# Values of two head groups in the second layer: computed in the order of positions, then reordered through memory

## The chip, the cores and the metric

One core of one Trainium2 chip runs the whole kernel. The metric is the device time of one execution in microseconds (us), of which the median of several runs is taken. TensorE (PE in the rows) does the matmuls, and each has a weight load ahead of it (PEld) that puts the 128x128 stationary operand into the array. VectorE is DVE, ScalarE is ACT, GpSimd is POOL, and SP is the queue from which this kernel issues all its transfers (DMA).

## The reference, cut to what matters

Four layers on 1024 positions of width 1024: gated linear attention, dilated sliding-window attention, differential attention and latent attention. The change is in the second. There the keys and values of three groups of heads come from the layer's input `x`, and each group attends on an interleaved subsequence of the positions:

```python
SWA_GROUPS = ((128, 1), (512, 4), (2048, 16))   # window, dilation
...
kv = x @ w_kv
k, v = jnp.split(kv, [SWA_KV_HALF], axis=-1)
...
def to_strided(t):        # t = i*d + r: subsequence r holds every d-th position
    ...
    t = t.reshape(bsz, n_sub, dilation, t.shape[2], e).transpose(0, 2, 1, 3, 4)
    return t.reshape(bsz, dilation, nb, blk, t.shape[3], e)
...
o = jnp.einsum('brngpqk,brnkge->brnqgpe', p, vcat) / ...
```

So group 0 wants the values of its 128-position blocks in plain order, group 1 those of every 4th position, and group 2 those of every 16th (the kernel takes every 8th, and masks half of them).

## The kernel before

Activations are held transposed: `xh` and `xl` are the two halves (high and low part) of the layer's input, 128 rows of the width on the partitions and the 1024 positions along the free dimension, for 8 slices `kt` of the width. A product in full precision is three matmuls, in `mm3` (lines 165 to 167): high by high, high by low, low by high.

The values are made by `u_v`: a block of 128 positions is the **stationary** operand (128x128, loaded into the array by PEld), and the weights `wvhi`, `wvlo` of the group (256 columns, two heads) are the moving one. A block takes 8 slices x 3 = 24 matmuls, and its result, 128 positions x 256, goes from PSUM (tile `mm`, two buffers) into `Vt[g][:, st, :]` by VectorE or ScalarE (line 953). For groups 1 and 2 `vsel` picks the block's 128 positions out of `x` with a step of 4 or 8 floats, so the stationary operand is read from SBUF with that step.

TensorE's order is the order in which the program is written (`manual_schedule`). It comes from `Fill`, a list of units that are cut into pieces and given out against a budget of time: three gate units, group 0's first four blocks and half of group 1's blocks run beside the tail of the boundary before (`before.tail`, a layer norm that writes the second 512 positions of `xh` and `xl`). Then come group 0's blocks 4 to 7, `ada[0]`, group 1's other four, `ada[1]`, group 2's first four, `ada[2]`, group 2's last four, `ada[3]`. An `ada` unit loads 2048 KB (`xa`, two buffers, line 554), weights it on VectorE into `xb` in eight steps (lines 563 and 565), sums it by two matmuls (line 571) and takes the result out on VectorE (lines 574 to 577).

The order on the other engines is set by a scheduler at build time. Every transfer stands in SP's queue, and one that waits there holds up all behind it. When the pool of the value stage (`swv`) is closed, the tables `C` and `Sn` (lines 975 and 976) of the rotation are loaded, and beside them a chain of small jobs starts: `xb<-in_lam` (617), `xb<-in_positions` (639), the tables of the third layer on VectorE (lines 642 to 658), and eight means of output weights (`wo`, lines 595 to 603, loaded, centred and stored one after the other in one buffer). The units of keys and queries then run; their results are rotated by VectorE from PSUM (line 899: `t<-mm,C`, which frees the PSUM buffer).

## Time and profile before

| | |
|---|---|
| median of 3 runs | 2852.13 us (2846.84 to 2853.86) |
| profiled execution | 2852.29 us, of which the span from the first to the last instruction is 2850.5 us |
| busy share of the span | PE 95%, PEld 80%, DVE 66%, ACT 47%, POOL 11% |
| mean granted TensorE clock | 0.983 of full speed |
| transfers | 270.51 MB, mean 95 GB/s |
| single steps on VectorE in the value stage | line 563 0.49 us, line 565 0.75, line 574 0.69, line 576 0.69, a block's copy out of PSUM (line 953) 0.42, a low part of weights (line 150, 128x512) 0.69 |

Busy shares are means over four layers with different limits. A row of the timeline gives the start in us from the span's start, the duration, the engine, the line of the source, the operation and the tiles (out<-in), and in brackets how long the engine stood idle before it and what ended that. Matmuls are pipelined, so the duration of one is longer than the distance to the next; the distance is what counts.

### The profile page before, as it was taken

To read this page: it belongs to the slowest core of one execution; us is meant where nothing else is said; L and a number is where in the kernel's file an instruction comes from. 1 tells how busy PE (TensorE), PEld (TensorE's weight loads), DVE (VectorE), ACT (ScalarE), POOL (GpSimd) and SP (SyncE) were. 2 spreads that over 40 slices of the span, in tenths; PEclk is the share of its full clock that TensorE was granted. 3 is DMA by queue.
4 is the path that set the end of the run, shared out by engine and by line. 5 is a ranking of instruction groups with operands and counts; after the bars stand their busy time and mean duration, and the time that the engine had idled before them with its cause. 6 is when DMAs were issued, how large, how long until landed. Compare 5 with 4: busy or idle time off the path is not lost.

```text
span 2850.5 us, 39300 instructions
## 1 busy us (share of the span) xinstructions
PE 2719.8 (95%) x14788; PEld 2287.2 (80%) x14788; DVE 1892.6 (66%) x3486; ACT 1347.4 (47%) x2498; POOL 314.5 (11%) x224
## 2 busy tenths in 40 slices
PE   8999999999999999989899999998899999999998
PEld 6889887898778878867787787876678778888888
DVE  5766647546666666666676688887676527776784
ACT  4443345404444434445714666665546514554563
POOL 0000000000000000000005566665100000000000
PEclk9999999999999999999999999999899999999999
DMA  5311146513211111145453333342185121110143
GB/s 178 115 41 45 45 150 203 187 71 137 87 49 42 49 53 45 45 156 169 162 207 106 53 59 61 69 65 50 44 299 181 48 93 32 29 29 29 39 168 108
DMA packets 161575, 270.51 MB, mean 95 GB/s; under 512 B 32773, under 2 KB 79141, under 8 KB 159849
## 3 DMA queue, kind: packets, MB, share of 16 engines
q1 hardware_dynamic: 161384, 268.00, 30.6%
q8 instruction: 116, 1.90, 0.3%
q14 instruction: 75, 0.61, 0.1%
HBM read 193.38 MB, written 64.07 MB: 90 GB/s over the span
## 4 chain that ended last, share of the span: by engine, by line
PE 63%; DVE 15%; DMA 8%; ACT 7%; issue 4%; SPq 2%; POOL 1%; ACTq 0%; DVEq 0%; POOLq 0%
PE mm L166 14%; PE mm L165 14%; PE mm L167 14%; PE pt L1226 3%; PE sc L1643 2%; PE sc L1406 2%; PE sc L1035 2%; DVE den L1410 1%; PE lv L477 1%; DMA zt<-zt 1%; PE pt L1139 1%; PE sc L166 1%; ACT whi L192 1%; PE sc L165 1%; PE sc L167 1%
## 5 line engine op out<-in xcount | busy, mean ns | idle before, releaser
L165 PE MATMUL mm<-xh,whi 128*128 128x512 f32 x1472 | 621.7, 422 | 12.7 <-ACT xh L763 4.3
L167 PE MATMUL mm<-xh,wlo 128*128 128x512 f32 x1472 | 582.3, 396 | 2.8 <-POOL wlo L150 1.8
L166 PE MATMUL mm<-xl,whi 128*128 128x512 f32 x1472 | 582.9, 396 | 1.7 <-DVE xl L150 1.7
L165 PEld LDWEIGHTS mm<-xh,whi 128*128 128x128 f32 x1472 | 281.9, 192 | 71.5 <-ACT xh L763 7.0
L167 PEld LDWEIGHTS mm<-xh,wlo 128*128 128x128 f32 x1472 | 280.3, 190 | 65.4 <-POOL wlo L150 2.2
L166 PEld LDWEIGHTS mm<-xl,whi 128*128 128x128 f32 x1472 | 281.5, 191 | 53.7 <-DVE xl L150 4.0
L150 POOL TENSOR_TENSOR wlo<-wraw,whi 128x1024 fp32r<-128x1024 f32 x29 | 70.4, 2427 | 1407.5 <-ACT whi L192 1406.8
L165 PE MATMUL mm<-wvhi,xh 128*128 128x256 f32 x704 | 220.2, 313 | 3.6 <-DVE V L953 3.0
L167 PE MATMUL mm<-wvhi,xl 128*128 128x256 f32 x704 | 215.0, 305 | 0.1
L166 PE MATMUL mm<-wvlo,xh 128*128 128x256 f32 x704 | 214.9, 305 | 0.0
L192 ACT CAST whi<-wraw 128x1024 fp32r<-128x1024 f32 (+2 forms) x141 | 135.9, 964 | 131.4 <-PE mm L166 124.8
L1412 ACT ACTIVATE P<-sc,den 128x1024 f32<-128x1024 f32 x128 | 142.8, 1116 | 105.5 <-DVE den L1410 105.5
L165 PEld LDWEIGHTS mm<-wvhi,xh 128*128 128x128 f32 x704 | 153.6, 218 | 8.4 <-DVE V L953 3.2
L166 PEld LDWEIGHTS mm<-wvlo,xh 128*128 128x128 f32 x704 | 153.8, 219 | 0.9 <-issue 0.7
L1410 DVE TENSOR_REDUCE den<-sc 128x1 f32<-128x1024 f32 x128 | 153.6, 1212 | 1.4 <-PE sc L1406 1.4
L167 PEld LDWEIGHTS mm<-wvhi,xl 128*128 128x128 f32 x704 | 153.6, 218 | 0.5 <-DVE xl L150 0.5
L150 DVE TENSOR_TENSOR wlo<-wraw,whi 128x1024 fp32r<-128x1024 f32 (+2 forms) x113 | 123.5, 1093 | 43.0 <-ACT whi L192 39.9
L1029 ACT ACTIVATE P<-P,nm 128x128 f32<-128x128 f32 (+1 forms) x192 | 84.9, 443 | 124.1 <-DVE nm L1027 123.8
L165 PE MATMUL mm<-oh,xh 128*128 128x512 f32 (+1 forms) x336 | 125.9, 375 | 0.3 <-ACT oh L784 0.2
L166 PE MATMUL mm<-ol,xh 128*128 128x512 f32 (+1 forms) x336 | 123.8, 369 | 1.4 <-DVE ol L150 1.4
L167 PE MATMUL mm<-oh,xl 128*128 128x512 f32 (+1 forms) x336 | 123.3, 367 | 0.0
L1039 DVE CUSTOM_DVE_ANT_0 P<-sc,band 128x128 f32<-128x128 f32 (+1 forms) x192 | 59.6, 348 | 71.8 <-PE sc L1035 71.3
(341 smaller groups left out, 6106.4 us busy)
## 6 DMA issues: line engine op xcount, KB each, us to landing
xa<-in_ada_w SPq DMA_DIRECT2D x12, 2048.0 KB
d_z<-zt SPq DMA_DIRECT2D x64, 256.0 KB
oh<-d_z SPq DMA_DIRECT2D x64, 256.0 KB
ol<-d_o SPq DMA_DIRECT2D x64, 256.0 KB
d_r<-X SPq DMA_DIRECT2D x48, 256.0 KB
wraw<-in_swa_wq SPq DMA_DIRECT2D x24, 512.0 KB
res<-d_r SPq DMA_DIRECT2D x40, 256.0 KB
zt<-zt SPq DMA_DIRECT2D x160, 64.0 KB
```

Of the source, the lines that this page charges most:

```text
L150: eng.tensor_tensor(out, src, hi.bitcast(F32), op=OP.subtract)
L165: mm(ps, l[0], r[0], start=first, stop=False)
L166: mm(ps, l[0], r[1], start=False, stop=False)
L167: mm(ps, l[1], r[0], start=False, stop=last)
L192: nc.scalar.copy(hi, raw)
L1029: S.activation(p[:, off:off + w_], p[:, off:off + w_], AF.Exp, bias=nm[:, g, b:b + 1], scale=scale, accum_out=stat(h, g, 1, b))
L1035: T.matmul(sc[:, b % 2, :w_], q[:, b * 128:b * 128 + 128], k[:, k0:k0 + w_], start=True, stop=True)
L1039: V.tensor_tensor_reduce(p[:, off:off + w_], sc[:, b % 2, :w_], mk, 1.0, NEG, op0=OP.add, op1=OP.max, accum_out=stat(h, g, 0, b))
L1226: nc.tensor.transpose(pt[:, i, :], P[:, (4 * j + i) * 128:(4 * j + i) * 128 + 128], self.ident)
L1406: T.matmul(sc[c][:, s], QS[h][c][r, q0:q0 + 128], (KL[h] if k else KH[h][c])[r, s], start=first, stop=not first)
L1410: V.tensor_reduce(dn[:, 2 + c:3 + c], sc[c], AX, OP.max, negate=True)
L1412: S.activation(p, sc[c], AF.Exp, bias=dn[:, 2 + c:3 + c], accum_out=dn[:, 1:2] if c else d0)
```

## The change

Groups 1 and 2 are computed in the order of positions, like group 0: `vsel` and the parameter `sel` go, and `u_v` reads 128 neighbouring positions. Each block of these groups is then written to memory (`d_s`, 128 KB, 16 of them). The reordered blocks are read back into the same tile `Vt[g]`, in rows of 256 floats: group 1 in two transfers of 512 KB, group 2 in one of 1024 KB. The order of group 1's blocks changes with it: 0 to 3 first, then 4 to 7, instead of the even ones and then the odd ones.

```diff
--- before.py
+++ after.py
@@ -227,7 +227,7 @@
                 u.pieces.append((lambda hf=hf, kt=kt: piece(hf, kt), 650))
         return u
 
-    def u_v(self, tag, wfn, evac, sts=range(8), x=None, kts=8, sel=None, per=1):
+    def u_v(self, tag, wfn, evac, sts=range(8), x=None, kts=8, per=1):
 
         u = Unit(tag, wfn)
         ps = {}
@@ -237,10 +237,7 @@
             if k0 == 0 and n % per == 0:
                 ps[0] = self.mmp.tile([128, per, 256], F32, name="mm")
             for kt in (k0, k0 + 1):
-                if sel is None:
-                    pick = lambda t: t(kt)[:, st * 128:st * 128 + 128]
-                else:
-                    pick = lambda t: sel(t(kt), st)
+                pick = lambda t: t(kt)[:, st * 128:st * 128 + 128]
                 self.mm3(ps[0][:, n % per, :], (pick(xh), pick(xl)), (u.w[0][:, kt, :], u.w[1][:, kt, :]), kt == 0,
                          kt == kts - 1)
             if k0 + 2 >= kts and n % per == per - 1:
@@ -298,6 +295,7 @@
             self.rsd = [self.dram(f"d_rs{i}", (1, 1024)) for i in range(8)]
             self.roped = self.dram("d_rope", (2, 128, 1024))
             self.vd = [self.dram(f"d_v{i}", (128, 8, 256)) for i in range(4)]
+            self.vs = [self.dram(f"d_s{i}", (1024, 256)) for i in range(2)]
             self.zd = [[self.dram(f"d_z{i}{j}", (128, 512)) for j in range(2)] for i in range(8)]
 
             self.mud = [self.dram(f"d_mu{i}", (1, 1024)) for i in range(2)]
@@ -933,13 +931,6 @@
             R = (None, msk[:, 4:8], msk[:, 16:24])
             Vt = [sp.tile([128, 8, 256], F32, name=f"V{g}") for g in range(3)]
 
-            def vsel(g):
-                if g == 0:
-                    return lambda t, b: t[:, b * 128:b * 128 + 128]
-                if g == 1:
-                    return lambda t, b: t.rearrange("p (i r) -> p r i", r=4)[:, b // 2, 128 * (b % 2):128 * (b % 2) + 128]
-                return lambda t, b: t.rearrange("p (i r) -> p r i", r=8)[:, b, :]
-
 
             with tc.tile_pool(name="swv", bufs=1, reuse_waits="tile") as vp:
                 pre = Fill()
@@ -950,19 +941,28 @@
                         w[g] = self.wwide(vp, A["swa_wv"][g], 2)
                     return w[g]
                 def u_vs(g, sts):
-                    u = self.u_v(None, lambda: wv(g), lambda st, ps: (S.copy if st % 2 else V.tensor_copy)(
-                        Vt[g][:, st, :], ps), sts=sts, sel=vsel(g))
+                    def evac(st, ps):
+                        (S.copy if st % 2 else V.tensor_copy)(Vt[g][:, st, :], ps)
+                        if g:
+                            nc.sync.dma_start(self.vs[g - 1][st * 128:st * 128 + 128, :], Vt[g][:, st, :])
+                        if g and st == 7:
+
+                            r = RES[g]
+                            for f in range(8 // r):
+                                nc.sync.dma_start(Vt[g].rearrange("p (r f) n -> p f r n", r=r)[:, f],
+                                                  self.vs[g - 1].rearrange("(f p r) n -> f p r n", p=128, r=r)[f])
+                    u = self.u_v(None, lambda: wv(g), evac, sts=sts)
                     u.early = g < 2
                     return u
 
                 pre.add(*[self.u_gate(h, "swa_wg", vp, (0,), before.w if h == 0 else None) for h in range(3)])
-                pre.add(u_vs(0, range(0, 4)), u_vs(1, range(0, 8, 2)))
+                pre.add(u_vs(0, range(0, 4)), u_vs(1, range(0, 4)))
                 for _ in before.tail:
                     pre.give(2240)
                 before.close()
                 with tc.tile_pool(name="ada0", bufs=1, side="right", reuse_waits="tile") as gp:
                     ada = [self.u_ada(gp, 0, t) for t in range(4)]
-                    pre.add(u_vs(0, range(4, 8)), ada[0], u_vs(1, range(1, 8, 2)), ada[1], u_vs(2, range(4)), ada[2],
+                    pre.add(u_vs(0, range(4, 8)), ada[0], u_vs(1, range(4, 8)), ada[1], u_vs(2, range(4)), ada[2],
                             u_vs(2, range(4, 8)), ada[3])
                     pre.drain()
             self.scales(0)
```

The number of matmuls and their order on TensorE stay the same. What moves is on SP, VectorE and ScalarE.

SP, from the last loads of group 0 and 1's weights (`wvraw`) to the loads of the rotation's tables, before:

```order
L203 DMA wvraw<-in_swa_wv 128x512 x3
L744 DMA d_mu<-rs 1x512
L554 DMA xa<-in_ada_w 128x4096 x3
L203 DMA wvraw<-in_swa_wv 128x512 x2
L554 DMA xa<-in_ada_w 128x4096
L975 DMA C<-in_swa_cos 128x1024
L976 DMA Sn<-in_swa_sin 128x1024
```

The same place in the change, up to the last load of `xa` (`V_4132` is group 1's tile):

```order
L203 DMA wvraw<-in_swa_wv 128x512 x3
L947 DMA d_s<-V_4132 128x256
L742 DMA d_mu<-rs 1x512
L552 DMA xa<-in_ada_w 128x4096 x2
L947 DMA d_s<-V_4132 128x256 x3
L552 DMA xa<-in_ada_w 128x4096
L203 DMA wvraw<-in_swa_wv 128x512 x2
L947 DMA d_s<-V_4132 128x256 x3
L552 DMA xa<-in_ada_w 128x4096
```

And on from there, to the loads that start the next stage (`V_4133` is group 2's tile):

```order
L952 DMA V_4132<-d_s 128x4x256
L947 DMA d_s<-V_4132 128x256
L947 DMA d_s<-V_4133 128x256 x2
L952 DMA V_4132<-d_s 128x4x256
L947 DMA d_s<-V_4133 128x256 x6
L952 DMA V_4133<-d_s 128x2048
L975 DMA C<-in_swa_cos 128x1024
L976 DMA Sn<-in_swa_sin 128x1024
L615 DMA xb<-in_lam 128x256
L623 DMA inv<-in_inv 128x2
L593 DMA wo<-in_swa_wo 128x1024
```

The last two loads of `xa` each stand behind three writes of group 1's blocks now, and the first load of the next stage, `C`, behind the last write and the reading back of group 2.

VectorE after the last `ada` unit, before (`t` and `sw` are the rotation of the first half of the first unit of keys, `t_5128` is its second half):

```order
L619 TENSOR_TENSOR xa<-xb 128x128
L899 TENSOR_TENSOR t_5096<-mm,C 128x512
L900 TENSOR_TENSOR sw<-sw,Sn 128x512
L621 TENSOR_REDUCE ls<-xa 128x2
L985 TENSOR_TENSOR K<-t_5096,sw 128x512
L642 CAST xa<-xb 128x512
...
L150 TENSOR_TENSOR wlo<-wraw,whi 128x1024
L648 SCALAR_TENSOR_TENSOR xa<-xa 128x512
L899 TENSOR_TENSOR t_5128<-mm,C 128x512
```

The same place in the change:

```order
L897 TENSOR_TENSOR t_5115<-mm,C 128x512
L898 TENSOR_TENSOR sw<-sw,Sn 128x512
L617 TENSOR_TENSOR xa<-xb 128x128
L985 TENSOR_TENSOR K<-t_5115,sw 128x512
L619 TENSOR_REDUCE ls<-xa 128x2
...
L640 CAST xa<-xb 128x512
...
L150 TENSOR_TENSOR wlo<-wraw,whi 128x1024
L644 TENSOR_SCALAR xa<-xa 128x512
L897 TENSOR_TENSOR t_5147<-mm,C 128x512
```

The rotation of the first half has moved ahead of the step that waits for `in_lam`. That of the second half still stands behind the cast that waits for `in_positions`.

## Rows read from the trace of the kernel before

**Rows 1.** Value-stage stretches, `mm` alone: us; PE, PEld, DVE, ACT busy (x); PEclk; DMA; GB/s.

```profile
550.22:573.67 23.45, 23.16 (x99) 22.86 (x98) 1.27 (x3) 0.37 (x1) 1.00 0.48 191
573.67:585.17 11.50, 11.50 (x97) 11.50 (x97) 1.27 (x3) 0.37 (x1) 1.00 0.22 61
585.79:608.31 22.52, 22.52 (x97) 22.52 (x97) 0.69 (x1) 1.12 (x3) 1.00 0.44 166
608.94:632.10 23.16, 23.16 (x97) 23.16 (x97) 1.54 (x3) 0.37 (x1) 1.00 0.00 1
632.73:656.19 23.46, 23.46 (x97) 23.46 (x97) 1.54 (x3) 0.37 (x1) 1.00 0.00 1
```

**Rows 2.** Groups of instructions, shapes apart, 550.3 to 573.4: busy, mean ns.

```profile
L167 PEld LDWEIGHTS mm<-wvhi,xl 128*128 128x128 f32 x32 | 10.7, 333 | 0.0
```

**Rows 3.** The same view, 573.7 to 585.

```profile
L167 PEld LDWEIGHTS mm<-wvhi,xl 128*128 128x128 f32 x32 | 6.0, 187 | 0.0
```

**Rows 4.** Timeline of PE, where group 0's block ends and group 1's begins.

```profile
550.10 0.28 PE L167 MATMUL mm<-wvhi,xl 128*128 128x256 f32 x1
550.22 0.40 PE L165 MATMUL mm<-wvhi,xh 128*128 128x256 f32 x1
550.46 0.40 PE L166 MATMUL mm<-wvlo,xh 128*128 128x256 f32 x1
```

**Rows 5.** Timeline of PE, in the first strided stretch and behind the plain one.

```profile
557.31 0.59 PE L741 MATMUL stat<-X,ones 128*128 128x512 f32 x1
...
585.17 0.59 PE L571 MATMUL mm<-xb,ones 128*128 128x512 f32 x1
```

**Rows 6.** Timeline of DVE at the end of the boundary before.

```profile
544.00 1.28 DVE L150 TENSOR_TENSOR xl<-X,xh 128x512 fp32r<-128x512 f32 x2
```

**Rows 7.** Timeline of SP, first loads of `xa`.

```profile
558.98 0.24 SPq L744 DMA_DIRECT2D d_mu<-rs  x1
559.32 0.82 SPq L554 DMA_DIRECT2D xa<-in_ada_w  x2
```

**Rows 8.** SP's own waits, 559 to 583: us in total, times, longest.

```profile
SPq L554 <- DMA xa<-in_ada_w: 6.8, 1, 6.8
```

**Rows 9.** Timeline of DVE, the first `ada` unit.

```profile
577.08 4.68 DVE L565 SCALAR_TENSOR_TENSOR xb<-xa,sc,xb 128x512 f32<-128x512 f32 x6
```

**Rows 10.** Timeline of SP at the start of the next stage.

```profile
656.43 0.33 SPq L975 DMA_DIRECT2D C<-in_swa_cos  x1
```

**Rows 11.** The chain of work, 656 to 667: start, us, what.

```profile
656.39 0.37 ACT V L953
...
657.33 5.38 DMA xb<-in_lam
...
663.06 3.11 DMA xb<-in_positions
```

**Rows 12.** Other transfers by way of memory in the chain of work: a write, a strided read.

```profile
712.53 2.89 DMA d_rope<-xa
...
1495.16 5.85 DMA vr<-d_v
```

**Rows 13.** Timeline of DVE there.

```profile
662.74 0.29 DVE L619 TENSOR_TENSOR xa<-xb 128x128 f32<-128x128 f32 x1 [3.67 <-DMA xb<-in_lam]
...
666.25 0.43 DVE L642 CAST xa<-xb 128x512 f32<-128x512 int32 x1 [0.24 <-DMA xb<-in_positions]
...
670.85 0.68 DVE L899 TENSOR_TENSOR t<-mm,C 128x512 f32<-128x512 f32 x1
```

**Rows 14.** Timelines of PE and ACT behind the value stage.

```profile
673.64 1.18 ACT L898 COPY sw<-mm 64x512 f32<-64x512 f32 x2 [3.45 <-PE mm L167]
725.38 1.52 PE L1035 MATMUL sc<-K,q 128*128 128x128 f32 x4 [2.45 <-DVE st L1039]
```

**Rows 15.** PE at 540 (timeline), and the stretch behind it: busy of all engines, PEclk.

```profile
539.99 0.39 PE L165 MATMUL mm<-wvhi,xh 128*128 128x256 f32 x1 [2.96 <-DVE V L953]
...
540.00:545.00 5.00, 5.00 (x29) 5.00 (x30) 5.00 (x8) 2.25 (x5) 0.00 (x0) 0.66 0.91 277
```

## Prediction, made before the changed kernel was run

> **What bounds the kernel now.** The page's busy shares come first (the table above): TensorE is busy nearly all the time, so time is to be had where its instructions take longer than they must, or where it waits. Next the stage that the change touches, cut into stretches at the units' borders [rows 1]. Each of the five stretches holds four blocks, that is 4 x 24 = 96 value matmuls (the first holds a pair of others too), and TensorE is busy from end to end. The one with plain blocks (group 0, 573.67 to 585.17) takes 11.50 us; the four with strided blocks take 23.45, 22.52, 23.16 and 23.46 us. The granted clock is 1.00 in all five, and transfers run at 191 GB/s in one slow stretch and at 1 GB/s in another, so neither clock nor transfers make the difference. The weights that move are a plain 256 columns in both, and so is the output. What differs is the stationary operand, and the groups show it: its load takes 333 ns with the step [rows 2], 187 ns without [rows 3]. At the border between the two kinds the distance between matmuls goes from 0.12 to 0.24 us from one instruction to the next [rows 4]. I read: with a step of 4 or 8 floats the load of the stationary operand, not the 256 columns, sets the pace.
>
> **What the change takes away.** 16 strided blocks become plain ones. The strided stretches add up to 23.45 + 22.52 + 23.16 + 23.46 = 92.59 us. The first is 0.93 us longer than its twin of the same group; I put 0.9 of that down to the pair of `stat` matmuls in it [rows 5], which stay. Four plain stretches are 4 x 11.50 = 46.0 us. Saving: 92.6 - 0.9 - 46.0 = 45.7 us, as long as TensorE stays fed.
>
> The Trainium skill says something that would deny this saving: in "TensorE: Matmul & The Clock Gate", section "Step-by-step: what each phase is for", the weights of the next tile load while the present matmul runs. By that alone a longer load costs nothing, and the change would only pay for its transfers. The trace agrees with the overlap for plain blocks (a load of 187 ns at a distance of 120 ns) but not for strided ones, where the distance grows with the load.
>
> **Is TensorE still fed?** In the value stage three things could now come late.
>
> (a) The second half of `xh`: VectorE writes its last slices at 544.00 [rows 6], and group 0's blocks 4 to 7, which need it, now start at 550.22 + 11.50 + 0.9 = 562.6.
>
> (b) The `ada` sums. The first `xa` load stands behind `d_mu` [rows 7], which needs the `stat` pair. That pair stood (557.31 - 550.22)/0.24 = 30 matmuls into its stretch; 30 at 0.12 are 3.6 instead of 7.1 us, so the load goes out 3.5 us earlier, at 555.8. SP saw the first `xa` land about 559.32 + 0.82 + 6.8 = 567 [rows 7, 8], 7.6 us after its issue; now at 563.4. VectorE's eight steps ended only at 577.08 + 4.68 = 581.8 [rows 9], because they queue behind copies out of PSUM. Six of them take 4.68, all eight about 6, so with the two copies between them they end near 570. The sum is due on TensorE at 562.6 + 11.5 = 574.1 (585.17 before [rows 5]): 4 us to spare. For the other three, an interval between two sums is 12.1 us now (11.5 + 0.6); VectorE needs (steps in the table above) 0.49 + 7 x 0.75 = 5.7 for the eight steps, 1.4 to take the sum out and 0.8 for two copies, and in one of the intervals 1.4 for two low parts of group 2's weights: 9.3 at most. The third and fourth `xa` now also wait for writes of blocks that TensorE finished earlier; both buffers are free by about 570 and 585, and 7.6 us later each has landed, before VectorE comes to it. Cost: 0, with 1 to 2 us at hand in the tightest interval; if that cover fails, 1 to 2 us in each of three intervals, 5 us in all.
>
> (c) PSUM: a block lasts 2.9 us, and group 0's blocks already run at that pace with the same two buffers. Cost 0.
>
> **What the change adds.** 16 writes of 128 KB and three readings, 2 MB each way. In the value stage they run beside transfers that leave room (1 GB/s in the last two stretches [rows 1]); the values are wanted only by the attention's products, far behind these rows. Their price lies in SP's queue, at the end. Let T be the end of the value matmuls, 656.19 in the trace. Before, `C` went out at T + 0.24 [rows 10]. Now ahead of it stand the last block's copy (done at T + 0.57 [rows 11]), its write, which must land, and the reading of group 2. The nearest write is 256 KB in 2.89 us from issue to landing [rows 12]: the reading goes out at T + 3.6 and `C` at about T + 4.2, 4.0 us later than before. The reading's 1 MB then lies ahead in the transfer queue. Two bounds: the first `xa`, 2 MB, landed 7.6 us after its issue and the write of 256 KB after 2.89, so 1.75 MB more take 4.7 us, and 1 MB in long runs 2.8 us; the strided read of 512 KB, in as many short runs as ours, landed after 5.85 us [rows 12], all of which may be ahead of `C`. I take 2.8, as our runs of 1 KB are twice as long. In all `in_lam` lands 4.0 + 2.8 = 6.8 us later, at T + 13.3 instead of T + 6.5 [rows 11, 13].
>
> Here the Trainium skill's "DMA: Bandwidth & Descriptors", section "Anatomy of one DMA", gives a fixed 2.0 us per transfer plus bytes at 436 GB/s. An estimate by it is 2.3 us for the write and 2.4 us for the reading's bytes, which would make `in_lam` 5.8 us late. The trace shows 2.89 us for twice the write's bytes.
>
> **What is late next.** `in_positions` goes out when VectorE has used `in_lam`, and lands 3.1 us later [rows 11]: T + 16.8 instead of T + 10.1. Behind that cast VectorE has 3.5 us of work until the rotation of the second half of the first keys (before: 666.25 to 670.85, 4.6 us [rows 13]), so this rotation reads its PSUM buffer at T + 20.3 and frees it at T + 20.9. TensorE wants that buffer after three halves, which ended at 673.6 before, T + 17.4 [rows 14]. Stall: 3.5 us. After 2.96 us of idleness the trace shows a mean granted clock of 0.66 for the 5 us that follow [rows 15]: (1 - 0.66) x 5 = 1.7 us at the lower level, 1.2 of 2.4 GHz. I add 1.5. The chain of `wo` loads begins about 7 us late too, 2 more than TensorE by then, and TensorE already waits on that chain's neighbours before, 2.45 us at 725 alone [rows 14]; I add 1.5. Sum: 6.5 us. Bounds: 0 if the scheduler's new order keeps VectorE off the path, 12 if the reading takes 5.85 us instead of 2.8, the lateness of then 10 us is paid in full, and one more fall of the clock comes with it.
>
> **Sum.** The profiled execution took 2852.29 us (span 2850.5), 0.16 over the median of the runs. 2852.3 - 45.7 + 6.5 = 2813.1; I predict 2813 us. By the estimate from the Trainium skill for the transfers the loss would be about 5.5 and the time 2812.
>
> **The rivals.**
> 1. *The transfers are hidden.* The second rotation isn't late enough, or TensorE doesn't need that PSUM buffer so soon: 2852.3 - 45.7 = 2806.6, or up to 2808. For it: VectorE stood idle 3.67 us before `in_lam` [rows 13]. Against: the cast is still ahead of the rotation in the new order.
> 2. *New waits eat more.* The `ada` intervals don't fit (5 us), or the chain is paid in full (12): 2818 to 2830. For it: 2 us to spare in 12, and the clock fell after the wait that ended at 539.99 [rows 15].
> 3. *No gain.* The load is hidden behind the matmul ahead of it and something else sets the distance; then only the cost is left: 2852.3 + 6.5 = 2858.8. Against: the load and the distance grow together, at one border [rows 1 to 4]. (This is the way it would go by the Trainium skill's sentence on overlap.)
> 4. *Slower.* The round trip through memory holds SP's queue for longer than the saving. The place is `C` behind the reading of group 2; every microsecond there beyond the 3 that VectorE has idle is paid once. It decides from 45.7 + 8.6 = 54 us of delay on; write and reading together show 2.89 + 5.85 = 8.7 us [rows 12]. Slower by over 0.3% would be 2861 or more.
>
> **How the numbers follow.** Forecast (2808.5 to 2818) 0.55, rival 1 (below 2808.5) 0.16, rival 2 0.23, rival 3 0.04, rival 4 0.02. The likeliest case gives 2813. The range leaves out rivals 3 and 4 and the outer ends of 1 and 2, whose bounds come from a loss of 0 and of 17 (5 + 12), with 3 us at the lower end because runs of this kernel differ by 7: 2804 to 2828. A measurement tells 0.3%, 8.6 us, from no change: faster 0.94 (forecast, rivals 1 and 2), same 0.04 (rival 3 for the most part), slower 0.02.
>
> **What would show it.** Right: the four stretches of groups 1 and 2 take 11.5 us each, their loads 187 ns; the last value matmul ends near 610.5; `C` is issued 4 us after that, and TensorE idles 3 to 4 us some 17 us later, with a granted clock below 1 behind it. Wrong: a distance above 0.12 us in these stretches; idle time of TensorE before the `ada` matmuls; or SP standing for more than 5 us at the reading of group 2.

## The result, and the profile after the change

| | before | after |
|---|---|---|
| median | 2852.76 us (2846.84 to 2853.86, 4 runs) | 2808.97 us (2801.23 to 2812.34, 4 runs) |
| profiled execution, span | 2852.29, 2850.5 us | 2811.72, 2809.9 us |
| mean granted TensorE clock | 0.983 | 0.981 |
| moved by transfers | 270.51 MB | 274.70 MB |

The ratio is 0.9847 with a 95% interval of 0.9825 to 0.9870: faster by 1.5%. 2813 us was predicted, with a range of 2804 to 2828.

First the stretches that answer to [rows 1], for `mm` alone with the same columns: group 1's first four blocks, group 0's last four, group 1's last four, group 2's two times four.

```profile
548.70:561.20 12.50, 12.21 (x99) 11.78 (x98) 0.85 (x2) 0.74 (x2) 1.00 0.57 209
561.20:572.70 11.50, 11.50 (x98) 11.50 (x97) 0.85 (x2) 0.74 (x2) 1.00 0.77 278
573.90:585.27 11.37, 11.37 (x96) 11.37 (x96) 1.44 (x3) 0.37 (x1) 1.00 0.42 156
586.27:597.64 11.37, 11.37 (x96) 11.37 (x96) 1.44 (x3) 0.37 (x1) 1.00 0.81 284
598.64:610.02 11.38, 11.38 (x96) 11.38 (x96) 1.44 (x3) 0.37 (x1) 1.00 0.15 48
```

96 matmuls take 11.4 us in every group now (the first row holds the pair of `stat` matmuls as well), whether transfers run at 48 or at 284 GB/s. The load of the stationary operand in the last of these stretches, shapes apart, which answers to [rows 2]:

```profile
L167 PEld LDWEIGHTS mm<-wvhi,xl 128*128 128x128 f32 x31 | 5.8, 187 | 0.0
```

Next, whether TensorE stayed fed. VectorE's last steps for the second `ada` sum, the sum on TensorE, and the step that takes it out:

```profile
582.77 1.53 DVE L563 SCALAR_TENSOR_TENSOR xb<-xa,sc,xb 128x512 f32<-128x512 f32 x2
...
586.17 0.69 DVE L572 TENSOR_TENSOR xb<-mm,ident 128x512 f32<-128x512 f32 x1 [1.86 <-PE mm L569]
...
585.11 1.02 PE L569 MATMUL mm<-xb,ones 128*128 128x512 f32 x2
```

VectorE ends at 584.3 and TensorE starts the sum at 585.11 without idle time: 0.8 us to spare in the tightest interval.

Then the price. SP at the end of the stage: the last six writes of 128 KB, the reading of group 2, and the loads behind it ([rows 10] before).

```profile
595.25 15.51 SPq L947 DMA_DIRECT2D d_s<-V  x6
612.26 0.32 SPq L952 DMA_DIRECT2D V<-d_s  x1
612.68 0.39 SPq L975 DMA_DIRECT2D C<-in_swa_cos  x1
...
613.59 0.71 SPq L615 DMA_DIRECT2D xb<-in_lam  x1
```

The last value matmul ends at 610.02, so `C` goes out 2.66 us behind it. Before the change the same matmul ended at 656.36 and `C` went out 0.07 us behind it; the 0.24 of the prediction counts from the start of the `ada` sum that follows it (656.19, now 609.85). The chain of work there ([rows 11] before): the last copy, its write, the two small loads, and the first store of the `wo` chain.

```profile
610.04 0.38 ACT V L945
610.44 1.68 DMA d_s<-V
...
613.59 9.05 DMA xb<-in_lam
...
622.98 3.15 DMA xb<-in_positions
...
627.85 3.65 DMA d_wo<-wo
```

VectorE, answering to [rows 13]: the step that waits for `in_lam`, the cast that waits for `in_positions`, the rotation of the second half.

```profile
622.66 0.29 DVE L617 TENSOR_TENSOR xa<-xb 128x128 f32<-128x128 f32 x1 [2.37 <-DMA xb<-in_lam]
...
626.21 0.43 DVE L640 CAST xa<-xb 128x512 f32<-128x512 int32 x1 [2.04 <-DMA xb<-in_positions]
...
629.55 0.68 DVE L897 TENSOR_TENSOR t<-mm,C 128x512 f32<-128x512 f32 x1
```

TensorE, its new waits above 1 us up to the first selection matmul (`sc<-xb,sel`, which needs the scores of all three groups), and the stretch behind the first of them, all engines:

```profile
630.29 0.50 PE L165 MATMUL mm<-xh,whi 128*128 128x512 f32 x1 [3.06 <-DVE t L897]
...
670.16 0.50 PE L165 MATMUL mm<-xh,whi 128*128 128x512 f32 x1 [1.28 <-DVE t L897]
...
699.95 0.71 PE L1035 MATMUL sc<-K,q 128*128 128x128 f32 x4 [2.22 <-DVE q L990]
...
717.97 0.66 PE L1095 MATMUL sc<-xb,sel 128*128 128x32 f32 x4 [3.18 <-DVE xb L1086]
...
630.00:635.00 5.00, 4.71 (x14) 3.73 (x15) 4.96 (x10) 1.17 (x2) 0.00 (x0) 0.66 0.75 223
```

TensorE waits 3.06 us for the second rotation to free its PSUM buffer, 17.2 us behind the last value matmul, and then runs five us at a mean clock of 0.66. Further on two waits of 1.28 and 2.22 us follow that were not there before. The wait of 2.45 us at 725 in [rows 14] has a counterpart of the same size (2.39 us at 683.7), and the last wait, for the selection itself, is 0.6 us longer than before (its row of before is below).

### The profile page after: what moved, and what is told of

Its sections match the earlier page's. It is cut to its first block, busy times and chain, and to the rows that moved or that the text cites. A ratio compares the mean times of both kernels' runs of the same rounds, so it can differ in the third digit from the quotient of the medians.

```text
span 2809.9 us, 39334 instructions
## 1 busy us (share of the span) xinstructions
PE 2672.6 (95%) x14788; PEld 2237.5 (80%) x14788; DVE 1892.4 (67%) x3486; ACT 1350.5 (48%) x2500; POOL 314.9 (11%) x224
## 2 busy tenths in 40 slices
DMA packets 165078, 274.70 MB, mean 98 GB/s; under 512 B 33076, under 2 KB 82516, under 8 KB 163224
## 4 chain that ended last, share of the span: by engine, by line
PE 64%; DVE 15%; DMA 8%; ACT 7%; issue 4%; SPq 1%; POOL 1%; ACTq 0%; DVEq 0%; POOLq 0%
PE mm L165 13%; PE mm L166 13%; PE mm L167 13%; PE pt L1226 3%; PE sc L1406 2%; PE sc L1643 2%; PE sc L1035 2%; DVE den L1410 1%; PE lv L475 1%; DMA zt<-zt 1%; PE pt L1139 1%; DVE wlo L150 1%; PE sc L166 1%; PE mm L1609 1%; PE mm L1607 1%
## 5 line engine op out<-in xcount | busy, mean ns | idle before, releaser
L165 PE MATMUL mm<-wvhi,xh 128*128 128x256 f32 x704 | 205.6, 292 | 3.6 <-DVE V L945 3.0
L167 PE MATMUL mm<-wvhi,xl 128*128 128x256 f32 x704 | 199.6, 284 | 0.1
L166 PE MATMUL mm<-wvlo,xh 128*128 128x256 f32 x704 | 199.2, 283 | 0.0
L165 PEld LDWEIGHTS mm<-wvhi,xh 128*128 128x128 f32 x704 | 134.7, 191 | 8.6 <-DVE V L945 3.2
L166 PEld LDWEIGHTS mm<-wvlo,xh 128*128 128x128 f32 x704 | 135.2, 192 | 1.5 <-issue 1.2
L167 PEld LDWEIGHTS mm<-wvhi,xl 128*128 128x128 f32 x704 | 134.4, 191 | 0.4 <-DVE xl L150 0.4
```

The lines of the kernel that those rows point to most:

```text
L165: mm(ps, l[0], r[0], start=first, stop=False)
L166: mm(ps, l[0], r[1], start=False, stop=False)
L167: mm(ps, l[1], r[0], start=False, stop=last)
```

## How the loss is measured below

A median of this kernel moves by several us from one set of runs to the next (the changed kernel gave 2808.97, 2815.94 and 2809.38), so a loss of 6 us is read from the traces: as the distance from the start of the last value copy on ScalarE (610.04 above, 656.39 in [rows 11]) to the first selection matmul. The latter's row before the change:

```profile
758.03 0.66 PE L1095 MATMUL sc<-xb,sel 128*128 128x32 f32 x4 [2.57 <-DVE xb L1086]
```

758.03 - 656.39 = 101.64 us before, 717.97 - 610.04 = 107.93 after: the price of the transfers is 6.3 us. What comes behind that matmul takes 2082 to 2096 us in the twelve profiles of the table, in no order of the variants: there lies the scatter that the distance leaves out.

TensorE in these two stretches, before and after, and in the kernel with a late reading (second time, below), all columns as in [rows 1] but for all tiles:

```profile
656.39:758.03 101.64, 95.01 (x421) 77.14 (x419) 76.46 (x190) 53.30 (x112) 0.00 (x0) 0.98 0.44 152
610.04:717.97 107.93, 95.39 (x420) 76.91 (x418) 76.82 (x190) 55.43 (x114) 0.00 (x0) 0.98 0.46 154
610.97:708.82 97.85, 93.25 (x420) 75.82 (x418) 76.12 (x190) 52.80 (x112) 1.69 (x3) 1.00 0.50 170
```

TensorE is busy for 95.0 and 95.4 us and idle for 6.6 and 12.5: of the 6.3 us, 5.9 are idle time. The mean granted clock is 0.98 in both, so the clock is no part of the price that shows, although it falls behind the new stall: before the change it fell once too, behind the wait of 2.45 us (first row), and there it does not fall after (second row):

```profile
724.38:734.38 10.00, 8.99 (x35) 7.41 (x36) 7.54 (x29) 7.85 (x22) 0.00 (x0) 0.83 0.54 213
...
682.70:692.70 10.00, 8.94 (x41) 7.36 (x42) 9.44 (x32) 6.83 (x18) 0.00 (x0) 1.00 0.39 125
```

In the table, "first `wo` store" is counted from the same copy, and "idle" is the distance less the time that TensorE is busy in it.

| kernel | median us | ratio to before (95%) | distance us | idle us | first `wo` store us |
|---|---|---|---|---|---|
| before |  |  | 101.6 | 6.6 | 11.6 |
| changed | 2809.0 | 0.9847 (0.9825 to 0.9870) | 107.9 | 12.5 | 17.8 |
| changed, second time | 2815.9 | 0.9868 (0.9843 to 0.9893) | 107.7 | 12.3 | 16.6 |
| changed, third time | 2809.4 | 0.9860 (0.9847 to 0.9874) | 107.5 | 12.2 | 16.3 |
| without transfers | 2804.1 | 0.9834 (0.9809 to 0.9858) | 101.4 | 6.4 | 11.5 |
| group 1 alone | 2829.9 | 0.9927 (0.9904 to 0.9950) | 101.9 | 7.2 | 12.2 |
| transfers alone | 2853.4 | 1.0015 (1.0003 to 1.0028) | 106.8 | 11.1 | 16.2 |
| group 2 in GpSimd's queue | 2810.3 | 0.9852 (0.9828 to 0.9875) | 104.3 | 9.3 | 17.5 |
| group 2 in one write | 2807.4 | 0.9851 (0.9827 to 0.9875) | 104.7 | 8.4 | 19.1 |
| late reading | 2805.6 | 0.9846 (0.9822 to 0.9870) | 98.6 | 5.2 | 11.9 |
| late reading, second time | 2799.5 | 0.9821 (0.9808 to 0.9835) | 97.9 | 4.6 | 11.8 |
| only the reading late | 2802.5 | 0.9836 (0.9823 to 0.9849) | 100.0 | 6.4 | 12.6 |

The second and the third time of the changed kernel were measured beside others on one chip each: the second with "without transfers", "GpSimd's queue" and "one write", the third with "transfers alone", "late reading, second time" and "only the reading late".

## Experiments

**Without the transfers, and the changed kernel again.** The edit:

```diff
-                        if g:
-                            nc.sync.dma_start(self.vs[g - 1][st * 128:st * 128 + 128, :], Vt[g][:, st, :])
-                        if g and st == 7:
...
```

> The changed kernel without its 16 writes and three readings: groups 1 and 2 keep the order of positions, so the reordering is left out of the computation. Theory (the changed kernel loses some 5 us behind the value stage, because C and in_lam stand behind the last write and the reading of group 2 in SP's queue): C goes out 0.2 to 0.3 us after the last value matmul as before the change, in_lam lands 6.5 us after it, TensorE has no idle time above 1 us in the 25 us that follow, and the time is 2804 (2809 less 5.3), 2802 to 2806. Rival (the loss comes from the shorter value stage itself: the loads of keys and of wo are late whatever stands in SP's queue): TensorE still idles 2 to 3 us there, and the time is 2808 to 2810. The four stretches of values take 11.4 us each by both.

> The changed kernel once more, beside the others on the same chip. 2809 (2804 to 2813); TensorE idles 3 us some 17 us behind the last value matmul in this profile too, and the granted clock falls behind it. Open: whether the clock falls behind the 3 us pause at 540, which is the same in both kernels: it fell before the change and did not after it. If that is chance, it can fall here.

Without the transfers SP sends `C` out at once and VectorE has `in_lam` 6 us behind the last copy (611.00):

```profile
611.04 0.33 SPq L967 DMA_DIRECT2D C<-in_swa_cos  x1
...
617.00 0.29 DVE L617 TENSOR_TENSOR xa<-xb 128x128 f32<-128x128 f32 x1 [3.32 <-DMA xb<-in_lam]
...
712.36 0.66 PE L1087 MATMUL sc<-xb,sel 128*128 128x32 f32 x4 [2.57 <-DVE xb L1078]
```

The distance is 712.36 - 611.00 = 101.4 us, and TensorE has no wait above 0.8 us in the 40 us behind the stage. The theory holds; the rival, that a shorter stage makes the next loads late by itself, falls. The repeat of the changed kernel missed what was expected of it: its median is 2815.9, its first stall 1.85 us and not 3, and the clock does not fall behind it. Yet the distance is again 107.7: the waits further on make up the difference. So no single stall is the price; it is the sum of TensorE's waits for late steps of VectorE.

**Group 1 alone.** In the kernel before, `vsel(1)` becomes `t[:, b * 128:b * 128 + 128]`, and group 1 gets its writes and readings:

```diff
-                    return lambda t, b: t.rearrange("p (i r) -> p r i", r=4)[:, b // 2, 128 * (b % 2):128 * (b % 2) + 128]
+                    return lambda t, b: t[:, b * 128:b * 128 + 128]
...
+                        if g == 1:
+                            nc.sync.dma_start(self.vs[g - 1][st * 128:st * 128 + 128, :], Vt[g][:, st, :])
...
```

> The kernel before with the change made for group 1 alone: its eight blocks plain, written and read back in two transfers; group 2 keeps its step of 8 floats and has no transfers. Theory (each plain stretch saves half, and only what stands in SP's queue at the end of the stage costs): group 1's two stretches take 11.4 us, group 2's two 23.2 to 23.5, the distance from the last value matmul to the first selection matmul stays 102 us, and the time is 2852.4 less 22.3, that is 2830 (2827 to 2833). Rival (each reading costs 2 to 3 us somewhere): 2833 to 2836.

2829.9 us against the 2830 expected (beside a kernel before of 2847.5 there, so the ratio of 0.9927 means 14 to 27 us saved where 22 were expected), and the distance stays at 101.9: group 1's half of the saving comes without a price in this stretch. Its transfers end long before the stage does.

**Transfers alone.** The kernel before with the 16 writes and three readings, but the steps kept:

> The kernel before with the 16 writes and three readings of the change, but with the blocks of groups 1 and 2 still read with their steps of 4 and 8 floats (the reordering is then done twice, so these values stand in the wrong order). Theory (the price of the transfers does not hang on the pace of the value matmuls): the strided stretches stay at 23 us, and the distance from the last value matmul to the first selection matmul is 108 us as in the changed kernel (108.11 and 107.87), against 101.95 in the kernel before, so 2852 + 6 = 2858, 2855 to 2861. Rival (slower blocks give the writes time to land, and the price falls): 102 to 104 us, 2852 to 2854.

The distance is 764.13 - 657.34 = 106.8 us, the ratio 1.0015 (1.0003 to 1.0028), which is 1 to 8 us. The median of 2853.4 lies below the 2855 to 2861 of the theory, but the kernel before took 2849.2 beside it; the distance decides for the theory, with 5.2 us where 6 were expected. So most of the price is there without the saving, and together with the run without transfers this separates the two terms of the forecast.

**Another place for group 2's transfers.** Two ways to let `C` go ahead. First all of group 2's transfers in GpSimd's queue:

```diff
+                        q = nc.gpsimd if g == 2 else nc.sync
                         if g:
-                            nc.sync.dma_start(self.vs[g - 1][st * 128:st * 128 + 128, :], Vt[g][:, st, :])
+                            q.dma_start(self.vs[g - 1][st * 128:st * 128 + 128, :], Vt[g][:, st, :])
...
```

> The changed kernel with the eight writes and the reading of group 2 issued from GpSimd's queue, which has nothing else to do in this stage; SP's queue then holds only group 1's. Theory (the wait in SP's queue is what costs): C goes out 0.3 us after the last value matmul instead of 2.7, no stall of 3 us behind it, 2804 to 2806. Rival 1 (the 1 MB of the reading costs, not its place: it shares the transfer engines with C, Sn and in_lam): C goes out early but in_lam lands 2 to 3 us later than before the change, the stall shrinks to 0 to 1 us, 2805 to 2808. Rival 2 (a transfer issued by GpSimd has a price of its own, or its writes land late): the reading lands later, but its values are wanted only after 740, so no more than 1 us.

Second, one write for the whole group:

```diff
-                        if g:
+                        if g == 1:
                             nc.sync.dma_start(self.vs[g - 1][st * 128:st * 128 + 128, :], Vt[g][:, st, :])
+                        elif g == 2 and st == 7:
+                            nc.sync.dma_start(self.vs[1].rearrange("(b p) n -> p b n", p=128), Vt[2])
```

> The changed kernel with group 2 written to memory in one transfer of 1024 KB after its last block instead of eight of 128 KB; with that the program's order puts C, Sn and in_lam ahead of the reading, right behind the issue of the write. So C waits for no landing, but 1 MB lies ahead of it in the transfer engines. Theory (two terms: the wait for the write's landing, 1.7 to 2.4 us, and the bytes of the reading ahead, 2.8 us): the first goes, the second stays, C goes out about 1.1 us after the last value matmul, in_lam lands 2 to 3 us earlier than in the changed kernel (10 us after the last value matmul instead of 12.6), the stall of 3.1 us falls below 1 us, and the time is 2805 to 2807. Rival (only the wait counts, bytes are shared fairly): in_lam lands 7 to 8 us after the last value matmul, no stall, 2804.

In both, `C` goes out within 0.9 us of the last copy and the stall 17 us behind it is gone. But the distance is 104.3 and 104.7: of 6.3 us, 2.6 and 3.1 stay, and come back for the most part as a wait near 698 (3.74 and 2.03 us; with one write the clock falls once more behind it). The times say less: 2810.3 is above what theory and rivals had told for GpSimd's queue, 2807.4 just above the theory for one write, beside a changed kernel of 2815.9 there, and the intervals of the three overlap. These are rows of the kernel with GpSimd's queue (last copy at 612.60): SP's wait for `in_lam`, which began at 614.9, the reading's issue, VectorE's first rotation, its step on `in_lam`, the issue of `in_positions`, and TensorE's wait for the last rotation of the queries.

```profile
SPq L637 <- DMA xb<-in_lam: 4.2, 1, 4.2
...
619.14 0.55 POOL L953 DMA_DIRECT2D V<-d_s  x1 [5.34 <-DMA inv<-in_inv]
...
620.14 0.69 DVE L897 TENSOR_TENSOR t<-mm,C 128x512 f32<-128x512 f32 x1 [4.88 <-ACT sw L896]
...
622.08 0.28 DVE L617 TENSOR_TENSOR xa<-xb 128x128 f32<-128x128 f32 x1
...
622.40 0.33 SPq L637 DMA_DIRECT2D xb<-in_positions  x1
...
697.84 0.71 PE L1036 MATMUL sc<-K,q 128*128 128x128 f32 x4 [3.74 <-DVE q L991]
```

The step on `in_lam` no longer waits for its load. `in_lam` landed at 614.9 + 4.2 = 619.1, 6.5 us behind the copy, as before the change, and the reading went out only then: up to here neither SP's queue nor the reading's bytes cost anything. But VectorE takes `in_lam` up at 622.08, because the step stands behind the rotation, which waits for ScalarE's copy of the first product; in the kernel before it stood ahead of it ([rows 13], at 662.74). So `in_positions` goes out 9.8 us behind the copy instead of 6.7, and the first `wo` store 17.5 instead of 11.6. The rotation stands ahead in every profile of the table that has group 2's reading at this place, and behind in every other, so where the reading stands changes the order that the build gives VectorE, and here that order alone held `in_positions` up by 3 us. What the order and the bytes of the reading cost behind that point is not separated. With one write it was different: there `in_lam` itself landed later, 9.2 us behind the copy, with the write's 1 MB ahead of it.

**A late reading.** So the reading has to be away from this place altogether. It stands behind the first scores, held there by a copy of one column that needs them, in GpSimd's queue:

```diff
+                        q = G if g == 2 else nc.sync
                         if g:
-                            nc.sync.dma_start(self.vs[g - 1][st * 128:st * 128 + 128, :], Vt[g][:, st, :])
-                        if g and st == 7:
+                            q.dma_start(self.vs[g - 1][st * 128:st * 128 + 128, :], Vt[g][:, st, :])
+                        if g == 1 and st == 7:
...
                 run([], [scores(0, g)], 1300)
+                if g == 0:
+                    G.tensor_copy(Vt[2][:, 0, 0:1], P[0][:, 0:1])
+                    G.dma_start(Vt[2].rearrange("p (r f) n -> p f r n", r=8)[:, 0],
+                                self.vs[1].rearrange("(f p r) n -> f p r n", p=128, r=8)[0])
```

> The changed kernel with group 2's eight writes in GpSimd's queue, and the reading of group 2 behind one small copy on GpSimd (128x1, into a place of group 2's tile that the reading overwrites) that waits for the first scores: so the reading can't start until some 36 us behind the last value matmul. Nothing of the change stands in SP's queue or in the transfer engines in the first 30 us then, and VectorE's order there is that of the kernel before. Theory (what is left of the loss when SP's queue is free, 2.5 to 3.9 us at the first selection matmul, comes from the reading being there at all: through its bytes, or through the order that the build gives VectorE because of it): the distance from the last value matmul to the first selection matmul is 101.5 to 102.5 us, as before the change (101.95) and without transfers (101.54), against 108 in the changed kernel, and the time is 2803 to 2805. Rival (the reading costs wherever it stands, because it takes transfer time from the loads of wo): 104 us and more, 2806 or more.

The first time gave a distance of 98.6 us, below what theory and rival had said, but a time of 2805.6 us, between the two, and with 0.9846 the ratio of the changed kernel's first time. So it was run again beside the changed kernel, with a variant whose eight writes stay in SP's queue:

> The kernel with the late reading again, beside the changed kernel on one chip. The distance from the last value matmul to the first selection matmul is 98.5 to 99.5 us, 9 us less than in the changed kernel; the medians differ by 3 to 10 us (2805.6 against 2809 and 2816 so far, with other runs of the kernel before beside them). Rival (the better order shows only in that stretch and is lost later on): the medians differ by less than 3 us.

> The changed kernel again, for that comparison: 108 us between the last value matmul and the first selection matmul, 2806 to 2814.

> As the late reading before, but group 2's eight writes stand in SP's queue, as in the changed kernel; only the reading is in GpSimd's queue and behind the first scores. C then stands behind the last write's issue, not behind its landing. The rows on VectorE are the same as with the writes on GpSimd. Theory (the reading alone is what costs): C goes out 0.9 us behind the last value matmul, the distance to the first selection matmul is 99 to 100 us (98.75 there), 2805 to 2807. Rival (what stands in SP's queue costs too): 102 us or more, 2808 or more.

The late reading, second time: GpSimd's copy and its transfer, VectorE's step on `in_lam`, and the selection matmul.

```profile
653.90 0.40 POOL L1200 COPY V<-P 128x1 f32<-128x1 f32 x1 [41.73 <-ACT P L1030]
654.68 0.76 POOL L1201 DMA_DIRECT2D V<-d_s  x1 [0.39 <-POOL V L1200]
...
617.48 0.29 DVE L617 TENSOR_TENSOR xa<-xb 128x128 f32<-128x128 f32 x1 [3.84 <-DMA xb<-in_lam]
...
708.82 0.66 PE L1096 MATMUL sc<-xb,sel 128*128 128x32 f32 x4 [2.57 <-DVE xb L1087]
```

The reading starts 43.7 us behind the last copy. `in_lam` is back at 6.5 us behind it and ahead of the rotation, and the distance is 97.9. On one chip 2799.5 (0.9821, 0.9808 to 0.9835) stands against the changed kernel's 2809.4 (0.9860, 0.9847 to 0.9874): the intervals don't touch, and this kernel beats the changed kernel by 10 us and the kernel before by 50. With the writes in SP's queue it is 2802.5 and 100.0 us, so by the distance the reading's place makes most of it and the writes' queue 1.5 to 2 us; the medians of these two don't tell them apart. The distance is even 3 to 4 us shorter than before the change. The rows say where that comes from: TensorE is idle for 4.6 us instead of 6.6 (the wait of 2.45 us in [rows 14] has become 0.85), and busy for 93.3 instead of 95.0, because the clock stays at 1.00 behind that shorter wait. Why VectorE's step comes earlier there is open.

**Two price lists.** The forecast rests on the pace that a step sets, so it was measured for each step. In the kernel before:

```diff
+                    return lambda t, b: t[:, 0:127 * (b + 1) + 1:b + 1]
...
+                if wstep:
+                    wp = lambda w: w.rearrange("p a b -> p (a b)")[:, 0:255 * (st + 1) + 1:st + 1]
```

> A price list; the values of groups 1 and 2 are wrong positions and weights, so that part of the computation is changed. In the kernel before, block b of group 1 reads its stationary operand with a step of b + 1 floats (1 to 8), and block b of group 2 reads a plain stationary operand and its moving one, 256 columns, with a step of b + 1 floats; no transfers. Theory A (a line of 16 bytes must be hit twice, as the Trainium skill's SBUF page states): steps of 1 and 2 load in 187 ns and run at 0.12 us, 4 to 8 load in 333 ns and run at 0.24, 3 lies between. Rival B (any step above 1 breaks the fast load): 2 and 3 cost the same 0.24 as 4. Rival C (it grows with the step, by the bytes passed over): 8 costs more than 4, which the rows of before with 0.235 and 0.242 hardly show. For the moving operand no row exists: by theory A the price for each element read is the load's, (333 - 187)/128 = 1.1 ns, so 256 columns take 0.12 + 0.29 = 0.41 us from step 4 on; by the opposite bound it costs nothing, 0.12.

Stretches inside single blocks, `mm` alone, columns as in [rows 1]: the stationary operand with steps of 1, 3, 4 and 8 floats, then the moving one with 1, 2, 4 and 8. The first count in brackets is the matmuls in the stretch, those that reach in over its edges included, so the distances of the table are taken from the starts of the matmuls of a block.

```profile
553.50:555.50 2.00, 2.00 (x19) 2.00 (x18) 0.00 (x0) 0.00 (x0) 1.00 0.47 124
...
560.00:563.00 3.00, 3.00 (x19) 3.00 (x18) 0.00 (x0) 0.06 (x1) 1.00 0.82 333
565.00:568.00 3.00, 3.00 (x15) 3.00 (x15) 0.00 (x0) 0.00 (x0) 1.00 1.02 437
...
598.40:603.70 5.30, 5.30 (x24) 5.30 (x23) 0.33 (x1) 0.00 (x0) 1.00 0.50 151
...
605.00:607.40 2.40, 2.40 (x23) 2.40 (x22) 0.62 (x1) 0.00 (x0) 1.00 0.73 314
608.00:612.80 4.80, 4.80 (x23) 4.33 (x22) 0.24 (x1) 0.00 (x0) 1.00 0.00 0
...
619.00:623.80 4.80, 4.80 (x23) 4.27 (x22) 0.28 (x1) 0.00 (x0) 1.00 0.00 0
...
641.40:646.00 4.60, 4.60 (x23) 4.34 (x22) 0.42 (x1) 0.00 (x0) 1.00 0.00 0
```

| step in floats | 1 | 2 | 3 | 4 | 5, 6, 7 | 8 |
|---|---|---|---|---|---|---|
| stationary: load ns | 188 | 198 | 262 | 330 | 320 to 331 | 338 |
| stationary: distance us | 0.12 | 0.12 | 0.175 | 0.23 | 0.23 | 0.24 |
| moving (256 columns): distance us | 0.12 | 0.23 | 0.23 | 0.23 | 0.22 to 0.23 | 0.22 |

For the stationary operand this is theory A: free up to a step of 2, half way at 3, full price from 4 on, whatever the bytes passed over. For the moving operand A fails at a step of 2, and its 0.41 us too: the price is there at once and stays at 0.23. The second list takes the moving weights in runs of neighbours:

> A second price list, for the moving operand, where a step of 2 floats doubled the distance already (0.12 to 0.23 us) and one of 8 cost no more, which the theory of 16-byte lines did not give. The values of groups 1 and 2 are computed with a plain stationary operand and with weights taken in runs of n floats out of every r (so they are products of wrong weights, and stand in plain order). Group 1, block by block: n of r = 1 of 1, 1 of 2, 2 of 4, 4 of 8, 8 of 16, 16 of 32, 32 of 64, 64 of 128; group 2: 2 of 8, 4 of 16, 8 of 32, 16 of 64, 32 of 128, 128 of 256, 1 of 8, plain. Theory P (two neighbouring floats are taken at once, so that a run of 2 is enough): 0.23 us for runs of 1, 0.12 for all others. Rival L (a line of 16 bytes at a time, all of it or at half pace): 0.23 for runs of 1 and 2, 0.12 from 4 on. Rival D (any pattern with a second dimension is slow): 0.23 for all but the plain ones.

These are the stretches with runs of 2 of 4, 4 of 8, 2 of 8, and 4 of 16 with 8 of 32:

```profile
560.00:565.00 5.00, 5.00 (x24) 4.53 (x23) 0.00 (x0) 0.37 (x1) 1.00 1.03 436
566.00:568.60 2.60, 2.60 (x25) 2.60 (x24) 0.42 (x1) 0.00 (x0) 1.00 1.06 454
...
593.80:598.80 5.00, 5.00 (x23) 4.47 (x22) 0.66 (x1) 0.00 (x0) 1.00 0.87 367
599.40:604.00 4.60, 4.60 (x40) 4.60 (x39) 0.38 (x1) 0.37 (x1) 1.00 0.00 0
```

Runs of 1 and of 2 floats cost 0.22 to 0.23 us, runs of 4 and more 0.12, with any gap: rival L. The moving operand wants four neighbouring floats, where the stationary one is content with a step of 2.

## Why the prediction was right

**The saving.** Counted from the end of the pause at 540 (539.99 in [rows 15], 540.13 after) to the last copy, the stage took 116.40 us and takes 69.91: 46.5 us less, where 45.7 were predicted. 1.5 of it is the clock, which fell behind that pause before the change and did not in this one execution; seven other profiles with the same value stage and a fall of the same length all show 71.4. At the same clock the saving is 45.0, 0.7 less than predicted. The premise, that the load with a step sets the pace, is what the list of steps shows: load and distance grow together from a step of 3 on. Rival 3 falls with it. So does, as a rule without a limit, the sentence on overlap in the Trainium skill's "TensorE: Matmul & The Clock Gate", section "Step-by-step: what each phase is for": loads of 187 and 198 ns are hidden at a distance of 0.12 us, loads of 262 ns and more are not.

**TensorE fed.** As predicted: no wait at an `ada` sum, 0.8 us to spare in the tightest interval (1 to 2 predicted; VectorE had four low parts of weights in it, not two). The first `xa` load goes out at 554.43 (555.8 predicted).

**The price.** 6.5 us were predicted and 6.3 measured. The path was right, as far as the rows reach: `C` behind the write, `in_lam` late, the second rotation late, a stall of TensorE. But the sizes of the terms were not, and the sum owes something to luck.

The write of 128 KB landed after 1.68 us, not 2.89, so `C` was held 2.6 us (2.66 - 0.07) and not 4.0. The prediction's estimate of 2.3 us by the Trainium skill's "DMA: Bandwidth & Descriptors", section "Anatomy of one DMA", is too long as well; by its heading that section is on transfers issued by GpSimd, and this one went out from SP. The reading's 1 MB was to cost the loads behind it 2.8 us (the two rows named give 4.7/1.75 = 2.7). In this execution `in_lam` was used 12.6 us behind the last value matmul (622.66 - 610.02) instead of 6.4, 6.3 later, so 3.7 go to the bytes. In the two repeats `in_lam` took less, 7.60 and 7.50 us from its issue instead of the 9.05 here and the 5.38 before, so there it is 2.2 and 2.1; one of them:

```profile
616.25 7.50 DMA xb<-in_lam
```

So the 6.8 us of lateness that were predicted were 6.3 once and 4.8 and 4.7 in the repeats. What hangs on it came nearly as told in the first profile: rotation at +19.7 (+20.3), stall of 3.06 (3.5) at +17.4 (+17.4), a lower clock behind it, all from the prediction's zero; in the repeats the stall was 1.85 and 1.51 us with the clock at 1.00 behind it. The distance was 107.7 and 107.5 all the same.

Two terms stood beside the stall. The 1.5 us for the clock added nothing: the stretch has one fall of the clock before and after, at another place (0.98 above). (The 1.7 us that the prediction calls time at the lower level is what a fall costs; the time at that level is twice as long.) The 1.5 us for the chain of `wo` loads stood for 2.9 us of further idle time (5.9 - 3.06), and for more in the repeats. That the `wo` chain carries it is not shown: TensorE's waits there end with rotations and other steps of VectorE, and the two variants with `C` sent early have their first `wo` store as late as the changed kernel, with distances 3 us shorter.

**The sum.** 46.5 - 6.3 = 40.2 us against 40.6 between the profiled executions; 1.5 of it is the clock behind the pause at 540, so at the same clock it would be 38.7, where 39.2 were predicted. Rival 1 (hidden) is refuted by the run without transfers, where the distance is 6.2 to 6.6 us shorter than in the three profiles of the changed kernel. Rival 4 falls with the time itself; SP waited at most 1.5 us for a write to land ahead of a reading. Of rival 2 no `ada` wait came up, and the 12 us of a chain paid in full were not reached.

**What the working missed** is the second way in which the reading acts. It named the queue and the bytes, and of VectorE's order only that the cast still stands ahead of the rotation. In the changed kernel itself the step on `in_lam` still waits for its load (2.37 us, 0.89 and 0.82 in the repeats), so there the order costs nothing at that step. But with the queue freed the order takes over, and only 3.2 to 3.7 of 6.3 us come back.

## What to carry to other kernels

When blocks differ only in how an operand is picked, compare the distance between matmuls across the border of two kinds: a busy TensorE can hide a factor of two, and a step of four floats in the stationary operand was such a factor here, with 256 columns moving. A round trip through memory that replaces the step was cheap here, where its values are wanted late, but its last wait fell on what starts the next stage: place the reading after that start, tied to something late, and read the new order of the other engines, because a scheduler can rearrange them around it. If an access pattern can be chosen, keep the stationary operand at a step of two floats at most, and the moving one in runs of four or more; these prices are for 128x128 stationary operands and 256 columns in this data type, and no run here shows others.

## What the runs showed of the hardware

The Trainium skill's "SBUF — State Buffer", section "Specifications (TRN2)", says that lines of 16 bytes need two hits each for full bandwidth. The stationary operand does just that (0.12 us at steps of 1 and 2, 0.23 from 4 on). The moving one does not: with two hits in a line, by a step of 2 or by pairs, it ran at 0.23. The measurement decides, and why the two differ is open.

The pause of 2.96 or 2.97 us ahead of the first value blocks is in all 14 profiles, but the granted clock fell behind it in 11 only. In 10 of these the mean over 536 to 552 is 0.89, which is 3.5 us at the lower level of 1.2 GHz, in one 0.79; in three (the changed kernel among them) it stayed at 1.00:

```profile
540.13 0.39 PE L165 MATMUL mm<-wvhi,xh 128*128 128x256 f32 x1 [2.96 <-DVE V L945]
...
536.00:552.00 16.00, 13.04 (x109) 12.83 (x108) 12.40 (x22) 8.27 (x15) 0.00 (x0) 1.00 0.77 248
```

Where the value stage is that of the changed kernel, it then takes 69.9 us without a fall, 71.4 with the usual one and 72.6 with the long one. So the same wait costs 0, 1.5 or 2.7 us from one execution to the next, and a single profile can't tell a change of that size.
